# Branch B's gated pair as seven half-size products in front of the heads, its convolution spread over the heads and branch A

## The chip, the core and the metric

The kernel runs on one core of one Trainium2 chip. The metric is the device time of one execution in microseconds (us). The core has a matrix engine (PE, with its own weight loads, PEld), a vector engine (DVE), a scalar engine (ACT) and a general engine (POOL); transfers are issued by SP and POOL through queues. Matrix products here are made of fp32 values split into a high and a low part (`hi`, `lo`, both of type fp32r), and each product is three passes: high by high, high by low, low by high.

## The reference, cut to what matters

512 tokens of 2048 channels go through one layer. Branch B takes two sets of 2048 columns of one large projection, gates one by the sigmoid of the other, and runs a causal convolution of 31 taps over the tokens of each channel:

```python
h = rmsnorm(x, g_pre[i])
proj = h @ w_in[i]
qkv, z_a, b_raw, a_raw, glu_in, z_b, gate_logits = jnp.split(proj, _split_points(), axis=-1)
...
o_a = gated_delta_chunked(q, k, v, g_log, beta)
o_a = rmsnorm(o_a, g_dn_out[i]).reshape(B, S, DN_WIDTH).astype(x.dtype) * jax.nn.silu(z_a)
y_a = o_a @ w_br_a[i]

u = jax.nn.glu(glu_in, axis=-1)
u = causal_depthwise_conv(u, w_dw[i]) + b_dw[i]
u = jax.nn.silu(layernorm(u, ln_g[i], ln_b[i])) * jax.nn.silu(z_b)
y_b = u @ w_br_b[i]

gate_a, gate_b = jnp.split(jax.nn.sigmoid(gate_logits + b_gate[i]), N_BRANCHES, axis=-1)
mixed = (gate_a * y_a + gate_b * y_b) @ w_out[i]
x = x + rmsnorm(mixed, g_post[i])
```

Behind it stands a gated per-layer embedding. `gated_delta_chunked` works on 16 heads of 128 channels in chunks of 64 tokens; each chunk needs the inverse of a 64x64 unit triangular matrix, and a state is carried from chunk to chunk.

## The kernel before

**Two kinds of product.** `gemm_cm` makes one tile of 128 output channels by 512 tokens: 16 pieces of depth 128, three passes each, 48 matmuls. Its weights come as two tiles of 128x1024 (`raw`, loaded by SP), and each half is split by ACT (`nc.scalar.copy`, L127) and DVE (subtraction, L128) into `w`. Seven half-size products in place of eight (Strassen's scheme in Winograd's form) make the projection `w_z` in `z_phase` and, at the end, `w_out`. A round `jp` of `z_phase` makes 512 tokens by 1024 columns: sums of weight blocks come from DVE (`e_a`, `e_b`) and from an accumulating transfer of POOL (`acc`), the sums of the left operand `S1` to `S4` are made once by `form`, and `run` issues the matmuls of two, three and two products, with DVE's additions of the results between them. The result has the tokens on the partitions; `fin` applies SiLU and stores it. There are two rounds. Column block 2jp + 1 of a round is complete after the second `run`, block 2jp after the third.

**The order of the program.** Embedding and transposition of x, five gate tiles, the two rounds of `z_phase`, the tile for beta and decay with its small steps (`beta_decay`), then the heads: eight groups of two heads. A group issues six products (k, q, v of two heads; each followed by a short convolution of four taps, `cv`, three DVE steps, L625) and two products of the queue `rest` (`zb_tile`, `gate_tile`). After the heads come a few more of `rest`, branch A (16 products with `w_br_a`), the layer norm of branch B, branch B's product, `w_out` and the embedding's gate.

**Small work beside the products.** Everything that isn't a product is a generator. `spawn` puts it into a list with a period; `tick` runs once for each matmul of `gemm_cm` and steps a generator whenever its count of matmuls has passed. A generator that yields a number waits for so many matmuls instead. This gives the program order; the build then fixes the order of each engine, with tiles granted from pools, and only instructions that are pinned (`pin`, L811) keep their program order exactly.

**A group of heads**, spawned with period HP = 4, goes through this chain: transposes of k, q, v on PE; `pg` on PE; W on DVE (L780); four copies `Ud` on ACT (L794); `UT` on DVE (L800); 31 pairs `prod` and `VT` on DVE (multiplication L811 and sum L812), which invert the triangular matrices column by column, each pair dependent on the one before; `Vd` (L819); four copies `VP` on ACT and four transposes `Tc` on DVE (L826); then `py` (L832) and `pz` (L835) on PE, which read `Tc`. From these the scan of the two heads follows.

**The gated pair of branch B** is `glu_pair(i)`, two `gemm_cm` products for each of 16 tiles of channels: the gate tile ends in a sigmoid (`evac_glu_b`), the value tile in a multiplication (`evac_glu_a`), and then `dwconv` is spawned with period CP = 6: a first tap on ACT, 30 dependent DVE steps of one tap each (L898, `uc`), the sum over channels `acc` on POOL and a store to `u_dram`. The first pair stands behind the heads, the second in front of branch A, the other 14 between branch A's products, each of which is also followed by one tile of `rest` as long as there are some. `presum`, spawned in branch A with period 10, makes sums of blocks of `w_out` by transfers on POOL's queue. `layer_norm` starts when all 16 channels' `u_dram` are stored.

## Time and profile before

| | us |
|---|---|
| median of 3 runs | 2472.0 (2471.88 to 2473.21) |
| the profiled execution | 2471.8 |
| its span in the trace | 2470.0 |

The span by stage, from the trace's busy times (us):

| stretch of the span | length | PE | DVE | ACT | POOL |
|---|---|---|---|---|---|
| 0 to 94.6: embedding, x, five gate tiles | 94.6 | 87.1 | 72.1 | 53.8 | 2.6 |
| 94.6 to 250.4: two rounds of `z_phase` | 155.8 | 155.6 | 118.9 | 83.0 | 10.2 |
| 250.4 to 1144: decay and the heads' groups up to the last `py` | 893.6 | 893.2 | 633.3 | 491.0 | 66.9 |
| 1144 to 1226: the last scan, tiles of `rest`, the first gated pairs | 82.0 | 82.0 | 57.5 | 42.7 | 12.1 |
| 1226 to 1825: branch A with the other pairs | 599.0 | 599.0 | 485.0 | 162.2 | 119.8 |
| 1825 to 2470: layer norm, branch B, `w_out`, embedding's gate | 645.0 | 633.4 | 378.3 | 275.9 | 7.2 |

In the prediction a row of the page's first part gives, for each engine, busy time, its share of the span and the number of instructions. A row that starts with two times and a colon is a stretch of the span: its length, then busy time and instructions of PE, PEld, DVE, ACT and POOL, the granted clock of PE, the share of time in which the DMA engines were busy, and GB/s. A row that starts with one time is a single instruction, or some alike behind each other: start, duration, engine, line, operation, output and inputs with shape; in brackets the idle time of the engine before it and what ended it. A row of costly groups ends in busy time, mean ns of one, and the idle time before. Rows with a queue name a kind of transfer, its count, size and the median us from issue to landing.

### The profile page before, as it was taken

How to read it: one execution, taken by the hardware profiler on the slowest of the kernel's cores; microseconds unless marked ns; L12 is line 12 of the kernel's file. 1: busy time of each engine (PE TensorE's matmuls, PEld its weight loads, DVE VectorE, ACT ScalarE, POOL GpSimd, SP SyncE). 2: the span in 40 equal slices, each digit the busy share in tenths (PEclk: the TensorE clock that was granted, in tenths of full speed). 3: DMA queues.
4: the chain of work that ended last, by engine and by line, in shares of the span. 5: the costliest groups of instructions: out<-in, count | busy, mean ns of one | idle time of the engine just before them, and what ended most of it. 6: DMA issues, size and time to landing. Idle time of an engine off the chain costs nothing.

```text
span 2470.0 us, 33169 instructions
## 1 busy us (share of the span) xinstructions
PE 2450.4 (99%) x12106; PEld 2019.3 (82%) x12106; DVE 1745.0 (71%) x3276; ACT 1108.5 (45%) x2165; POOL 218.7 (9%) x291
## 2 busy tenths in 40 slices
PE   8999999999999999999999999999999999999998
PEld 7888888888888888888888888888888888788886
DVE  7877767777686776766886877868975755667644
ACT  6555565555645556564422222222224723444532
POOL 0001100100000010000222322310000000000000
PEclk9999999999999999999999999999999999999999
DMA  7576432223232222323676866853353633565552
GB/s 267 171 184 176 126 115 86 98 86 99 73 103 90 86 99 86 99 69 116 180 220 184 234 203 184 237 161 111 104 186 123 209 118 108 213 232 168 197 170 77
DMA packets 131460, 361.31 MB, mean 146 GB/s; under 512 B 14816, under 2 KB 23264, under 8 KB 131296
## 3 DMA queue, kind: packets, MB, share of 16 engines
q1 hardware_dynamic: 112096, 310.94, 37.7%
q0 software_dynamic: 18048, 46.15, 8.1%
q10 hardware_dynamic: 1152, 2.10, 0.3%
q8 instruction: 95, 1.56, 0.3%
q14 instruction: 69, 0.57, 0.1%
HBM read 310.90 MB, written 48.23 MB: 145 GB/s over the span
## 4 chain that ended last, share of the span: by engine, by line
PE 97%; DVE 1%; issue 1%; DMA 1%; ACT 0%; SPq 0%; POOL 0%; DVEq 0%; POOLq 0%; ACTq 0%
PE g L183 24%; PE g L185 24%; PE g L181 23%; PE zp L431 2%; PE zp L429 2%; PE zp L430 2%; PE f L1247 2%; PE f L1248 2%; PE f L1246 2%; PE f L1412 2%; PE f L1411 2%; PE f L1410 2%; PE psB L678 1%; PE psS L684 1%; PE psA L672 1%
## 5 line engine op out<-in xcount | busy, mean ns | idle before, releaser
L183 PE MATMUL g<-hl,w 128*128 128x512 f32 x2064 | 815.6, 395 | 0.0
L185 PE MATMUL g<-hh,w 128*128 128x512 f32 x2064 | 815.3, 395 | 0.0
L181 PE MATMUL g<-hh,w 128*128 128x512 f32 x2064 | 813.6, 394 | 0.0
L127 ACT CAST w<-raw 128x512 fp32r<-128x512 f32 x716 | 438.5, 619 | 732.9 <-PE g L185 626.9
L128 DVE TENSOR_TENSOR w<-raw,w 128x512 fp32r<-128x512 f32 x716 | 503.1, 707 | 281.5 <-ACT w L127 279.3
L185 PEld LDWEIGHTS g<-hh,w 128*128 128x128 f32 x2064 | 388.2, 188 | 77.0 <-DVE w L128 2.7
L183 PEld LDWEIGHTS g<-hl,w 128*128 128x128 f32 x2064 | 388.1, 188 | 76.8 <-issue 1.6
L181 PEld LDWEIGHTS g<-hh,w 128*128 128x128 f32 x2064 | 388.3, 188 | 74.5 <-issue 0.5
L898 DVE SCALAR_TENSOR_TENSOR uc<-sg,vec,uc 128x511 f32<-128x511 f32 (+14 forms) x480 | 351.1, 733 | 14.0 <-ACT uc L895 3.9
L625 DVE SCALAR_TENSOR_TENSOR cv<-g,vec,cv 128x511 f32<-128x511 f32 x144 | 106.1, 737 | 29.0 <-ACT cv L623 28.2
L181 PE MATMUL g<-oh,w 128*128 128x512 f32 x256 | 99.6, 389 | 0.0
L183 PE MATMUL g<-ol,w 128*128 128x512 f32 x256 | 99.6, 389 | 0.0
L185 PE MATMUL g<-oh,w 128*128 128x512 f32 x256 | 99.6, 389 | 0.0
L181 PE MATMUL g<-uh,w 128*128 128x512 f32 x256 | 99.6, 389 | 0.0
L183 PE MATMUL g<-ul,w 128*128 128x512 f32 x256 | 99.6, 389 | 0.0
L185 PE MATMUL g<-uh,w 128*128 128x512 f32 x256 | 99.6, 389 | 0.0
L811 DVE TENSOR_TENSOR prod<-UT,VT 128x2 f32<-128x2 f32 (+30 forms) x248 | 87.2, 352 | 6.6
L966 POOL DMA_DIRECT2D wsum<-in_w_out x96 | 75.4, 850 | 75.0 <-issue 28.5
L1247 PE MATMUL f<-wsp,oph 128*128 128x512 f32 x192 | 75.4, 393 | 0.1
L1246 PE MATMUL f<-wsp,oph 128*128 128x512 f32 x192 | 75.4, 394 | 0.0
L1410 PE MATMUL f<-w,xh 128*128 128x512 f32 x192 | 75.4, 392 | 0.0
L1248 PE MATMUL f<-wsp,opl 128*128 128x512 f32 x192 | 75.2, 392 | 0.0
(363 smaller groups left out, 3386.3 us busy)
## 6 DMA issues: line engine op xcount, KB each, us to landing
raw<-in_w_in SPq DMA_DIRECT2D x258, 512.0 KB, 3.3
wsum<-in_w_out POOLq DMA_DIRECT2D x96, 256.0 KB, 5.7
raw<-in_w_ple_gate SPq DMA_DIRECT2D x40, 512.0 KB, 3.4
raw<-in_w_br_a SPq DMA_DIRECT2D x32, 512.0 KB, 3.8
wo_sums<-wsum POOLq DMA_DIRECT2D x64, 256.0 KB, 4.1
raw<-in_w_br_b SPq DMA_DIRECT2D x32, 512.0 KB, 3.3
raw<-in_w_z SPq DMA_DIRECT2D x22, 512.0 KB, 4.3
rw<-wo_sums SPq DMA_DIRECT2D x20, 512.0 KB, 4.3
```

The source lines that it names most:

```text
L127: nc.scalar.copy(hi, rq)
L128: nc.vector.tensor_tensor(lo, rq, hi.bitcast(F32), ALU.subtract)
L181: mm(ps, wh, rh, start=(k == 0), stop=False)
L183: mm(ps, wh, rl, start=False, stop=False)
L185: mm(ps, wl, rh, start=False, stop=(k == NK - 1))
L625: nc.vector.scalar_tensor_tensor(y[:, s:], ps[:, 0:T - s], vv(w0 + 3 - s), y[:, s:], ALU.mult, ALU.add)
L811: pin(nc.vector.tensor_tensor(pv_, um, vm, ALU.mult))
L898: nc.vector.scalar_tensor_tensor(y[:, s:], u[:, 0:T - s], vv(w0 + TAPS - 1 - s), y[:, s:], ALU.mult, ALU.add)
L1246: mm(ps, lh, wh[:, c], start=kk == 0, stop=False)
L1247: mm(ps, lh, wl[:, c], start=False, stop=False)
L1248: mm(ps, ll, wh[:, c], start=False, stop=kk == 7)
L1410: mm(ps[tt], lh, wh, start=k == 0, stop=False)
```

## The change

The columns of the gated pair get a copy in the layout of `w_z` (`w_glu`): four blocks of 1024 columns, the left half values, the right half their gates. `z_phase` runs four more rounds on them, with the same left operand. In these, the right half of the result goes through the sigmoid on ACT, and the left half is multiplied by it on DVE. The gated value has the tokens on the partitions, and the convolution needs the channels there: `transposed` makes 64 transposes of 128x128 on PE into 16 tiles `ut`, copies them out with ACT (`u0`) and stores them to `u0_dram`, 32 transfers of SP. It runs beside the next round's first products, and for the last round behind the phase.

`glu_pair` and its 32 products are gone. `dwconv` loads its channels from `u0_dram` (SP); its 30 steps (now L909) are the same. Channels 0 to 7 are convolved one after the other as a generator that is spawned behind the tile for beta and decay and ends with the heads, one step each 12 matmuls; channels 8 to 15 as one that is spawned in front of branch A, with a step after 4 and 5 matmuls by turns. `acc` is added on DVE in place of POOL. `rest` is taken in another rhythm: six tiles behind the heads, three in front of branch A, seven after branch A's products and the others later. `presum` goes at period 8 with pauses of 19 in place of 10 and 24.

```diff
-        WZ = A["w_z"]
+        blocks = [(A["w_z"], 0), (A["w_z"], 1)] + [(A["w_glu"], j) for j in range(4)]
...
-            nc.sync.dma_start(raw, WZ[jp, blk, q])
+            nc.sync.dma_start(raw, blocks[jp][0][blocks[jp][1], blk, q])
         def acc(t, jp, blk, q):
-            nc.gpsimd.dma_start(t, WZ[jp, blk, q], accum_op=ALU.add)
+            nc.gpsimd.dma_start(t, blocks[jp][0][blocks[jp][1], blk, q], accum_op=ALU.add)
...
-        for jp in range(2):
+        for jp in range(6):
...
-        for jp in range(2):
+        def transposed(cb, halves_):
+            yield
+            yield
+            for half, two in enumerate(halves_):
+                for c2 in range(2):
+                    ps = gps.tile([P, T], F32, tag="g", name="ut")
+                    for n in range(4):
+                        c = 2 * c2 + n // 2
+                        nc.tensor.transpose(ps[:, n * P:(n + 1) * P], two[n % 2][:, c * P:(c + 1) * P], ident)
+                    yield
+                    o = unit_s("u0")
+                    nc.scalar.copy(o, ps)
+                    for n in range(2):
+                        nc.sync.dma_start(u0_dram[cb + 2 * c2 + n][:, half * 256:half * 256 + 256], o[:, n * 256:n * 256 + 256])
+                    yield
+        for jp in range(6):
+            glu = jp >= 2
             ps = run(("P1", "Q5"), stepper(gen, 2))
+            for _ in gen:
+                pass
...
             for t in range(2):
                 tt_(d[t], ps["P3"][t], d[t], ALU.add)
-                fin(t, 2 * jp + 1, d[t])
                 tt_(s5[t], s5[t], u2[t], ALU.subtract)
-                fin(2 + t, 2 * jp + 1, s5[t])
+                for n, c in ((0, d[t]), (2, s5[t])):
+                    if glu:
+                        nc.scalar.activation(c, c, AF.Sigmoid)
+                    else:
+                        fin(n + t, 2 * jp + 1, c)
             ps = run(("P2", "Q4"))
             for t in range(2):
                 tt_(s1[t], ps["P2"][t], s1[t], ALU.add)
-                fin(t, 2 * jp, s1[t])
                 tt_(u2[t], ps["Q4"][t], u2[t], ALU.add)
-                fin(2 + t, 2 * jp, u2[t])
+                for n, c, g in ((0, s1[t], d[t]), (2, u2[t], s5[t])):
+                    if glu:
+                        tt_(c, c, g, ALU.mult)
+                    else:
+                        fin(n + t, 2 * jp, c)
+            gen = transposed(4 * (jp - 2), (s1, u2)) if glu else iter(())
         finish("form")
         ctx_z.close()
+        spawn(gen, 6)
...
+    cpool = [slots, "s"]
+    def dwconv(i):
+        w0 = V_DW + i * TAPS
+        u = cpool[0].tile([P, T], F32, tag=cpool[1], name="u")
+        nc.sync.dma_start(u, u0_dram[i])
+        yield
+        y = cpool[0].tile([P, T], F32, tag=cpool[1], name="uc")
+        nc.scalar.activation(y, u, AF.Identity, scale=vv(w0 + TAPS - 1), bias=vv(V_BDW + i))
+        yield
+        for s in range(1, TAPS):
+            nc.vector.scalar_tensor_tensor(y[:, s:], u[:, 0:T - s], vv(w0 + TAPS - 1 - s), y[:, s:], ALU.mult, ALU.add)
+            yield
+        if i == 0:
+            acc.append(slots.tile([P, T], F32, tag="s", name="acc"))
+            nc.gpsimd.tensor_copy(acc[0], y)
+        else:
+            nc.vector.tensor_tensor(acc[0], acc[0], y, ALU.add)
+        nc.sync.dma_start(u_dram[i], y)
+        done[0] += 1
+    def convs(channels, waits):
+        n = 0
+        for i in channels:
+            for _ in dwconv(i):
+                yield waits[n % len(waits)]
+                n += 1
+    CONV_H = 8
+    jobs.append(lambda: spawn(convs(range(CONV_H), (12,)), 12, "heads"))
...
-        else:
-            nc.gpsimd.tensor_tensor(acc[0], acc[0], y, ALU.add)
...
-    def evac_glu_a(i):
-        def f(ps):
-            u = sg_t.pop(i)
-            nc.vector.tensor_tensor(u, ps, u, ALU.mult)
-            spawn(dwconv(i, u), CP)
-        return f
-
-    def glu_pair(i):
-        gemm_cm(w_in_tile(GLU_TILE0 + 16 + i), hT, evac_glu_b(i))
-        gemm_cm(w_in_tile(GLU_TILE0 + i), hT, evac_glu_a(i))
-
-    for i in range(4):
+    for i in range(6):
         rest.popleft()()
-    glu_pair(0)
...
-                yield 24
+                yield 19
                 yield from give(a, T2)
                 yield from take(a, B21, True)
-                yield 24
+                yield 19
-    rest.popleft()()
-    glu_pair(1)
+    jobs.append(lambda: spawn(convs(range(CONV_H, NK), (4, 5)), 4, "conv"))
+    for _ in range(3):
-    jobs.append(lambda: spawn(presum(), 10, "presum"))
-    nglu = 2
-        if i + 5 < NK:
+        if i < 7:
             rest.popleft()()
-        if nglu < NK:
-            glu_pair(nglu)
-            nglu += 1
...
-    t = w.reshape(2, 4, 2, P, 2, 2, T).transpose(4, 0, 5, 1, 3, 2, 6)
+    t = w.reshape(2, 4, 2, P, -1, 2, T).transpose(4, 0, 5, 1, 3, 2, 6)
...
+        "w_glu": _sw_tiles(np.concatenate([glu[:, n * D + j * T:n * D + (j + 1) * T] for j in range(4) for n in range(2)], axis=1)),
```

The build's order shows where the convolution now stands. Rows are instructions of one engine in its own order: line, operation, output and inputs by name, shape; line numbers are those of the kernel that is shown. The first place is DVE in the fourth group of heads, in the second half of the inversion. `prod` and `VT` are the inversion's pairs, `w` is the split of a weight half for PE. Before:

```order
L812 TENSOR_REDUCE VT<-prod 128x6
L128 TENSOR_TENSOR w<-raw,w 128x512
L811 TENSOR_TENSOR prod<-UT,VT 128x132
L812 TENSOR_REDUCE VT<-prod 128x6
L811 TENSOR_TENSOR prod<-UT,VT 128x138
L812 TENSOR_REDUCE VT<-prod 128x6
L811 TENSOR_TENSOR prod<-UT,VT 128x144
L812 TENSOR_REDUCE VT<-prod 128x6
L811 TENSOR_TENSOR prod<-UT,VT 128x175
```

And with the change, from the same pair on, `uc` being a step of the convolution:

```order
L840 TENSOR_REDUCE VT<-prod 128x6
L909 SCALAR_TENSOR_TENSOR uc<-u,vec,uc 128x508
L839 TENSOR_TENSOR prod<-UT,VT 128x132
L909 SCALAR_TENSOR_TENSOR uc<-u,vec,uc 128x507
L840 TENSOR_REDUCE VT<-prod 128x6
L128 TENSOR_TENSOR w<-raw,w 128x512
L839 TENSOR_TENSOR prod<-UT,VT 128x138
L909 SCALAR_TENSOR_TENSOR uc<-u,vec,uc 128x506
L840 TENSOR_REDUCE VT<-prod 128x6
L909 SCALAR_TENSOR_TENSOR uc<-u,vec,uc 128x505
L839 TENSOR_TENSOR prod<-UT,VT 128x144
```

Before, `VT` is followed by the next `prod` at once, but for one `w`; with the change a step `uc` stands behind nearly every `prod` and every `VT` of this piece.

The second place is DVE behind the inversion, in the same group: `Vd`, then `Tc`, which PE reads in `py` and `pz`. Before:

```order
L819 STREAM_TRANSPOSE Vd<-VT 128x256
L625 SCALAR_TENSOR_TENSOR cv<-g,vec,cv 128x511
L128 TENSOR_TENSOR w<-raw,w 128x512
L625 SCALAR_TENSOR_TENSOR cv<-g,vec,cv 128x510
L826 STREAM_TRANSPOSE Tc<-VP 32x8x32
L625 SCALAR_TENSOR_TENSOR cv<-g,vec,cv 128x509
L826 STREAM_TRANSPOSE Tc<-VP 32x8x32 x3
```

With the change:

```order
L909 SCALAR_TENSOR_TENSOR uc<-u,vec,uc 128x499
L847 STREAM_TRANSPOSE Vd<-VT 128x256
L128 TENSOR_TENSOR w<-raw,w 128x512
L854 STREAM_TRANSPOSE Tc<-VP 32x8x32 x4
L909 SCALAR_TENSOR_TENSOR uc<-u,vec,uc 128x498
L128 TENSOR_TENSOR w<-raw,w 128x512
```

The three `cv` between `Vd` and `Tc` have moved ahead of `Vd`; the `w` has stayed, and the four `Tc` follow one another. On PE nothing has moved between `pg` and `py` in this group: 190 matmuls `g` and the one `pe` stand there before and with the change.

The third place is DVE in branch A. `gt` is the evacuation of a product of branch A. Before, a product of branch A, a pair of products for the gated pair and the convolution run side by side:

```order
L950 TENSOR_TENSOR gt<-g,gt 128x512
L128 TENSOR_TENSOR w<-raw,w 128x512
L898 SCALAR_TENSOR_TENSOR uc<-sg,vec,uc 128x500
L898 SCALAR_TENSOR_TENSOR uc<-sg,vec,uc 128x499
L898 SCALAR_TENSOR_TENSOR uc<-sg,vec,uc 128x498
L128 TENSOR_TENSOR w<-raw,w 128x512
L898 SCALAR_TENSOR_TENSOR uc<-sg,vec,uc 128x497
L898 SCALAR_TENSOR_TENSOR uc<-sg,vec,uc 128x496
L898 SCALAR_TENSOR_TENSOR uc<-sg,vec,uc 128x495
```

With the change:

```order
L909 SCALAR_TENSOR_TENSOR uc<-u,vec,uc 128x492
L909 SCALAR_TENSOR_TENSOR uc<-u,vec,uc 128x506
L970 TENSOR_TENSOR gt<-g,gt 128x512
L128 TENSOR_TENSOR w<-raw,w 128x512
L909 SCALAR_TENSOR_TENSOR uc<-u,vec,uc 128x491
L909 SCALAR_TENSOR_TENSOR uc<-u,vec,uc 128x505
L909 SCALAR_TENSOR_TENSOR uc<-u,vec,uc 128x490
L128 TENSOR_TENSOR w<-raw,w 128x512
L909 SCALAR_TENSOR_TENSOR uc<-u,vec,uc 128x489
L909 SCALAR_TENSOR_TENSOR uc<-u,vec,uc 128x504
L909 SCALAR_TENSOR_TENSOR uc<-u,vec,uc 128x488
L909 SCALAR_TENSOR_TENSOR uc<-u,vec,uc 128x503
```

Two channels' steps now alternate where one channel's steps followed each other, and three or four stand between two `w` where three stood; the steps of channels 0 to 7 have left this stage, and so have the products of the gated pairs.

More of the change, by code (lines that the diff above doesn't have):

```diff
@@ L267, in _body @@
     zb_dram = dram.tile([NK, P, T], F32, name="zb_dram")
+    u0_dram = dram.tile([NK, P, T], F32, name="u0_dram")
     def gate_tile(i, src=True):
@@ L363, in load @@
                 for n in range(2):
-                    nc.sync.dma_start(two[n], WZ[jp, blk, q][:, n * T:(n + 1) * T])
+                    nc.sync.dma_start(two[n], blocks[jp][0][blocks[jp][1], blk, q][:, n * T:(n + 1) * T])
                 return two
             raw = rawp.tile([P, 1024], F32, tag="raw", name="raw", bufs=3)
-            nc.sync.dma_start(raw, WZ[jp, blk, q])
+            nc.sync.dma_start(raw, blocks[jp][0][blocks[jp][1], blk, q])
             return [raw[:, 0:T], raw[:, T:]]
         def acc(t, jp, blk, q):
-            nc.gpsimd.dma_start(t, WZ[jp, blk, q], accum_op=ALU.add)
+            nc.gpsimd.dma_start(t, blocks[jp][0][blocks[jp][1], blk, q], accum_op=ALU.add)
         def parts(t):
@@ L864, in group @@
             yield wait
+    u_t = [None] * NK
+    done = [0]
+    acc = []
+    cpool = [slots, "s"]
[25 more added lines that the diff above has]
+    jobs.append(lambda: spawn(convs(range(CONV_H), (12,)), 12, "heads"))
     rest = deque([lambda i=i: zb_tile(i) for i in range(NK)] + [lambda i=i: gate_tile(i) for i in range(FILL, NK)]
@@ L989, in load_gate @@
         nc.sync.dma_start(mixed[i], g_dram[i])
-    rest.popleft()()
-    glu_pair(1)
+    jobs.append(lambda: spawn(convs(range(CONV_H, NK), (4, 5)), 4, "conv"))
+    for _ in range(3):
+        rest.popleft()()
     jobs.append(lambda: finish("oa"))
@@ L995, in _body @@
         jobs.append(lambda i=i: load_gate(i))
-    jobs.append(lambda: spawn(presum(), 10, "presum"))
-    nglu = 2
+    jobs.append(lambda: spawn(presum(), 8, "presum"))
     for i in range(NK):
```

27 lines of the change are left out of this document (2 added, 25 removed).

## The prediction

> **What bounds the kernel now.** I read the page's busy times first, then the chain of work that ended last, then the busy times by stage.
>
> ```profile
> PE 2450.4 (99%) x12106; PEld 2019.3 (82%) x12106; DVE 1745.0 (71%) x3276; ACT 1108.5 (45%) x2165; POOL 218.7 (9%) x291
> PE 97%; DVE 1%; issue 1%; DMA 1%; ACT 0%; SPq 0%; POOL 0%; DVEq 0%; POOLq 0%; ACTq 0%
> 94.00:250.00 156.00, 155.76 (x675) 126.32 (x674) 119.08 (x195) 82.58 (x141) 10.15 (x19) 1.00 0.64 178
> 670.00:714.00 44.00, 44.00 (x203) 35.86 (x201) 34.20 (x92) 22.80 (x29) 1.38 (x2) 1.00 0.31 102
> 714.00:778.00 64.00, 64.00 (x443) 53.34 (x442) 42.50 (x103) 36.02 (x112) 5.89 (x7) 1.00 0.26 83
> 1400.00:1600.00 200.00, 200.00 (x884) 165.68 (x883) 158.06 (x228) 54.91 (x88) 56.55 (x78) 1.00 0.75 212
> ```
>
> PE is the bound: 99% busy, 97% of the chain, no stage with idle PE. So work taken off PE is time won, as long as no engine that feeds PE falls behind. The rows by stage (PE, PEld, DVE, ACT, POOL) show who could: DVE. In branch A (1400 to 1600) 884 matmuls start in 200 us, one each 0.226 us; a matmul's own 0.39 us overlaps the next and is not its price.
>
> The average hides one place. A group of two heads holds an inversion, and its run on DVE is this:
>
> ```profile
> 678.97 1.25 DVE L800 STREAM_TRANSPOSE UT<-Ud 128x1024 f32<-128x1024 f32 x1 [6.87 <-ACT Ud L794]
> ...
> 709.06 0.67 DVE L819 STREAM_TRANSPOSE Vd<-VT 128x256 f32<-128x256 f32 x1
> ...
> 712.62 1.38 DVE L826 STREAM_TRANSPOSE Tc<-VP 32x256 f32<-32x256 f32 x3
> ...
> 713.88 0.69 PE L832 MATMUL py<-Tc,W 32*32 32x32 f32 x32
> 714.50 0.68 PE L835 MATMUL pz<-W,Tc 64*64 64x64 f32 x16
> ```
>
> DVE idles 6.87 us for ACT's copies, starts UT at 678.97, works through to Vd at 709.06 (30.1 us) and ends the last Tc at 714.00. PE reads Tc in py and pz, and pz starts at 714.50. PE was not idle, but the spare is 0.50 us. From UT to the last Tc DVE, not PE, has no room.
>
> **The change part by part.** I sum against the profiled execution, 2471.8 us (span 2470.0), 0.2 us under the median of 2472.0.
>
> Removed: 32 products of 48 matmuls, 1536 x 0.2262 = 347.5 us of PE.
>
> Added: four rounds of seven half-size products, 336 matmuls each, of the kind that the z phase has twice.
>
> ```profile
> L429 PE MATMUL zp<-w,hh x66: 389/397/398, 94.6 to 249.6; 128*128 128x512 f32 x66
> L431 PE MATMUL zp<-w,hl x66: 389/393/397, 95.0 to 250.0; 128*128 128x512 f32 x66
> L258 PE MATMUL xp<-cst,x 128*128 128x128 f32 x64 | 8.4, 274 | 0.0
> ```
>
> The z phase's 672 matmuls run from 94.6 to 250.4 with the seams between rounds in it: 155.8 us, 0.232 us each, so 1344 cost 311.7 us. The 64 transposes are as many and as large as those of x: 8.4 us. PE is left 347.5 - 311.7 - 8.4 = **27.4 us** less. In these rounds DVE gets about the z phase's load (119 of 156 us), four multiplications a round more; ACT (83 of 156) and DMA (0.64) have room for the extra copies. If that cover failed I would bound it by what a round lost so far, 77.9 - 336 x 0.2262 = 1.9 us, once more for four rounds: 0 to 8 us; I take 0, because the row's own price holds the seams.
>
> Moved: the convolution, 30 dependent DVE steps a channel. Eight channels go into the heads, eight into branch A, and their order is what matters. In a steady group (third to seventh) the run from UT to Vd has 12 splits w and 3 steps cv before; now 14 w, 6 cv and 13 steps uc stand there (the rows of the change's section are a piece of it). What one costs there, start to start:
>
> ```profile
> 693.42 0.28 DVE L812 TENSOR_REDUCE VT<-prod 128x6 f32<-128x126 f32 x1
> 693.62 0.68 DVE L128 TENSOR_TENSOR w<-raw,w 128x512 fp32r<-128x512 f32 x1
> 694.22 0.40 DVE L811 TENSOR_TENSOR prod<-UT,VT 128x132 f32<-128x132 f32 x1
> 694.66 0.29 DVE L812 TENSOR_REDUCE VT<-prod 128x6 f32<-128x132 f32 x1
> ...
> 697.86 0.74 DVE L625 SCALAR_TENSOR_TENSOR cv<-g,vec,cv 128x511 f32<-128x511 f32 x1
> 698.52 0.68 DVE L128 TENSOR_TENSOR w<-raw,w 128x512 fp32r<-128x512 f32 x1
> 699.12 0.74 DVE L625 SCALAR_TENSOR_TENSOR cv<-g,vec,cv 128x510 f32<-128x510 f32 x1
> ```
>
> A w takes 0.60 us, a cv 0.66; uc is the same instruction on the same width, 0.66. An independent step behind a VT starts 0.08 us before its end, a dependent one 0.04 after (694.22 + 0.40 to 694.66), so each dependent pair that is parted gives 0.12 back; 20 more are parted. Sum: 13 x 0.66 + 3 x 0.66 + 2 x 0.60 - 20 x 0.12 = 9.4 us on a run that had no gap. Behind Vd the three cv are gone, and the four Tc then follow ACT's copies as in the last group, which has no cv either:
>
> ```profile
> 1109.41 1.25 DVE L800 STREAM_TRANSPOSE UT<-Ud 128x1024 f32<-128x1024 f32 x1 [6.86 <-ACT Ud L794]
> ...
> 1137.79 0.67 DVE L819 STREAM_TRANSPOSE Vd<-VT 128x256 f32<-128x256 f32 x1
> ...
> 1141.32 0.44 DVE L826 STREAM_TRANSPOSE Tc<-VP 32x256 f32<-32x256 f32 x1 [0.28 <-ACT VP L825]
> ```
>
> 3.97 us from Vd to the last Tc's end, where a steady group has 4.94: 1.0 us back. PE's side has not moved: 190 matmuls and pe between pg and py, before and after. So pz comes 9.4 - 1.0 - 0.5 = **7.9 us late in a steady group**. Nothing covers it: py heads PE's queue, and every weight product stands behind it. The second group has 14 uc, 15 w and two matmuls more: 8.4. In the first, 26 uc, 19 w and 12 cv add 21.8 us by the same prices, and 53 more matmuls (12.0 us) lie before py: 21.8 - 12.0 - 1.0 - 0.5 = 8.3. The last has no uc. Heads: 5 x 7.9 + 8.4 + 8.3 = **56 us**. The lower bound is half of it, should DVE start its run earlier than in any group seen; the upper adds the rest of each group. There 17 uc and 0.66 us each make 11 us beside 42.5 of 64: 84%, and in the order most stand where DVE waits for PE. I take nothing; at most one step's 0.66 us at a few places, 3 us a group, 20 in all.
>
> Between the z phase and the first group the decay's small steps meet 30 uc (20 us):
>
> ```profile
> 250.00:298.00 48.00, 47.90 (x217) 39.05 (x216) 32.04 (x69) 24.11 (x38) 8.44 (x7) 1.00 0.40 121
> 298.00:347.00 49.00, 48.72 (x244) 39.46 (x244) 34.20 (x59) 32.31 (x71) 7.59 (x8) 1.00 0.39 126
> ```
>
> 66 + 20 of 97 us fits on average, not in every piece; 0 to 8 us, and I take 3.
>
> Branch A: two products (96 matmuls, 21.7 us) now have 25 uc, 8 w and one evacuation or acc: 25 x 0.65 + 8 x 0.60 + 0.68 = 21.7. DVE is exactly full for 20 products. The weights run three pieces ahead (a piece lasts 12 x 0.226 = 2.7 us), so 8 us of lag show nothing: 0 to 10 us, I take 1. The presum is stepped faster, 198 ticks (44.8 us) for a q instead of 248.
>
> ```profile
> wsum<-in_w_out POOLq DMA_DIRECT2D x96, 256.0 KB, 5.7
> wo_sums<-wsum POOLq DMA_DIRECT2D x64, 256.0 KB, 4.1
> ```
>
> Its longest dependent line is four loads and three stores, 4 x 5.7 + 3 x 4.1 = 35 us, which still fits. But it now lasts into the layer norm, and there rst on POOL, gate evacuations on ACT and loads on SP's queue stand behind its landings, with DVE's dg and PE's weights behind them in turn: 0 to 15 us, I take 1, since 35 is well under 44.8.
>
> Sum: 2471.8 - 27.4 + 56.2 + 3 + 1 + 1 = 2505.6, so **2506 us**.
>
> **The rivals.** *The cover holds, faster.* If the 13 steps cost PE nothing, because DVE finishes Tc before py after all, the time is 2471.8 - 27.4 + 5 = 2449. For it speaks that PE never idled in the heads and most uc stand harmlessly; against it the 0.50 us. The point that decides is 9.4 us of added work against 1.5 us of room. Chance 0.16.
>
> *The stall is smaller.* Half of it, 28 us: 2478. It needs room that seven groups lack: 0.09, about half of it within 0.2% of no change.
>
> *The clock drops in the stalls.* Here the two ends of the trace speak:
>
> ```profile
> 7.78 0.63 PE L213 MATMUL e_ps<-w,ph 128*128 128x512 f32 x1
> 8.20 0.63 PE L214 MATMUL e_ps<-w,ph 128*128 128x512 f32 x1
> ...
> 10.68 0.39 PE L214 MATMUL e_ps<-w,ph 128*128 128x512 f32 x1
> 2460.00:2464.00 4.00, 0.71 (x4) 0.23 (x2) 2.10 (x6) 1.57 (x6) 0.55 (x1) 1.00 0.01 2
> 2465.00:2467.00 2.00, 0.00 (x0) 0.00 (x0) 1.31 (x2) 0.00 (x0) 0.00 (x0) 0.50 0.95 327
> ```
>
> The granted clock (the third column from the right) was 1.00 through 2464 and 0.50 from 2465 on, some 4 us after the last two matmuls, and the first matmuls started 0.42 us apart until 10.68. A stall that long would cost ten matmuls 0.2 us each, 2 us; seven of them 14: 2520. A late stall is broken up, since the last splits in the run are late too: by my sums some 1 us, 1.5 us, then 4 us before py and 0.8 before pz, just at the limit. Chance 0.21. [...]
>
> *Branch A or the layer norm stalls.* DVE full or the presum late by the upper bounds above, 10 to 25 us on top: 2523. No wait of that kind is in the trace; chance 0.12.
>
> *The change doesn't do what it says*: the built order shows it does, so nothing is kept for this.
>
> **How the numbers follow.** The forecast keeps 0.42. The range leaves out the faster case (0.16) and a little above its end: 2478 to 2530. A measurement of this kernel can't tell less than about 0.2%, 5 us, from no change. Faster by more than that 0.16, within it 0.05, slower 0.79.
>
> **What would show it.** Right: PE idle in front of py and pz in seven groups, 6 to 9 us each, put down to DVE's Tc, with uc between prod and VT and no idle time on DVE; a group of about 115 us instead of 107.6 (four groups lie between the UT rows at 678.97 and 1109.41); rounds of 78 us in the longer z phase; branch A without idle PE. Wrong: a group that keeps 107.6 us; idle PE mainly in the rounds of seven products or behind the presum's landings; a granted clock under 1.00 inside the heads, which would be the third rival.

## The result, and the profile after

| | before | with the change |
|---|---|---|
| median, us | 2472.07 (2471.88 to 2473.21) | 2538.25 (2537.08 to 2545.23, 4 runs) |
| the profiled execution | 2471.8 | 2545.2, the longest of the four |
| its span | 2470.0 | 2543.4 |

The ratio is 1.0273 (1.0254 to 1.0291): slower by 66 us, 32 us beyond the forecast and 8 beyond the range's upper end.

The page's busy times and its chain of work that ended last, with the change:

```profile
PE 2469.7 (97%) x11978; PEld 2010.4 (79%) x11978; DVE 1861.4 (73%) x3539; ACT 1183.5 (47%) x2299; POOL 222.1 (9%) x292
PE 72%; DVE 19%; issue 4%; DMA 3%; ACT 2%; SPq 0%; POOL 0%; DVEq 0%; POOLq 0%; ACTq 0%
```

PE has 128 instructions fewer and is busy 19 us longer, and a quarter of the chain runs through other engines. What PE waited for, by the view of its waits (total us, times, longest):

```profile
PE py L860 <- DVE Tc L854: 33.9, 12, 5.2
PE g L185 <- DVE w L128: 7.3, 9, 1.2
```

One wait of 5.2 us stands in each steady group. PE's timeline in the fourth group shows it (start, duration, engine, line, operation; in brackets the idle time ahead and who ended it):

```profile
1084.40 0.39 PE L183 MATMUL g<-hl,w 128*128 128x512 f32 x1
1089.95 0.28 PE L860 MATMUL py<-Tc,W 32*32 32x32 f32 x2 [5.16 <-DVE Tc L854]
1090.53 1.06 PE L860 MATMUL py<-Tc,W 32*32 32x32 f32 x30 [0.30 <-DVE Tc L854]
1091.52 2.33 PE L863 MATMUL pz<-W,Tc 64*64 64x64 f32 x32
1093.77 0.79 PE L185 MATMUL g<-hh,w 128*128 128x512 f32 x1
1094.36 0.63 PE L181 MATMUL g<-hh,w 128*128 128x512 f32 x1
...
1097.35 0.55 PE L183 MATMUL g<-hl,w 128*128 128x512 f32 x1
1097.74 0.40 PE L185 MATMUL g<-hh,w 128*128 128x512 f32 x1
```

and DVE's timeline, what PE waited for. DVE has no idle time of 0.1 us or more from UT (1048.68) to Vd, and behind Vd only 0.15 to 0.24 us ahead of each Tc, for ACT's copy:

```profile
1086.41 0.71 DVE L128 TENSOR_TENSOR w<-raw,w 128x512 fp32r<-128x512 f32 x1
1087.02 0.44 DVE L840 TENSOR_REDUCE VT<-prod 128x8 f32<-128x256 f32 x1
1087.35 0.75 DVE L909 SCALAR_TENSOR_TENSOR uc<-u,vec,uc 128x499 f32<-128x499 f32 x1
1087.99 0.65 DVE L847 STREAM_TRANSPOSE Vd<-VT 128x256 f32<-128x256 f32 x1
...
1091.38 0.44 DVE L854 STREAM_TRANSPOSE Tc<-VP 32x256 f32<-32x256 f32 x1 [0.24 <-ACT VP L853]
```

That is the forecast's stall, at its place. But PE's matmuls behind it start 0.43 us apart instead of 0.23 until 1097.4. The busy times by stretch have the granted clock in the third column from the right:

```profile
1086.00:1087.00 1.00, 0.00 (x0) 0.00 (x0) 1.00 (x2) 0.30 (x1) 0.00 (x0) 1.00 0.00 0
1087.00:1088.00 1.00, 0.00 (x0) 0.00 (x0) 1.00 (x4) 0.00 (x0) 0.00 (x0) 0.72 0.85 279
1088.00:1090.00 2.00, 0.05 (x2) 0.08 (x2) 1.65 (x4) 1.30 (x2) 0.70 (x1) 0.50 0.31 123
...
1096.00:1097.00 1.00, 1.00 (x4) 0.73 (x3) 0.88 (x2) 0.00 (x0) 0.00 (x0) 0.50 0.00 0
1097.00:1098.00 1.00, 1.00 (x5) 0.80 (x4) 0.00 (x0) 0.00 (x0) 0.00 (x0) 0.66 0.00 0
1098.00:1099.00 1.00, 1.00 (x7) 0.55 (x5) 0.10 (x1) 0.82 (x2) 0.00 (x0) 1.00 0.00 0
```

The clock fell to half 2.6 us into the wait (1087.44) and stayed there for 10.2 us, far into the work behind it. Added up over the span in stretches of one or two microseconds, PE had 75 us at half clock between the rounds and branch A; before the change, none.

By stage, from matmul starts: the rounds of seven products 476.6 us instead of 155.4; from their end to branch A's first product 1069.0 instead of 976.5; branch A 255.8 instead of 598.2; from its last product to w_out's first 296.8, unchanged.

The following table is worked out from each trace, from the start of pg's last matmul and of py's first; it carries most of the verdicts below. "pg to py" and "py to next pg" are a steady group's (third to seventh) in us, "half" the time at half clock in one such group. The first two groups with the change differ: 13.7 us at half clock in each, and 3.4 more in the first.

| kernel | median, us | pg to py | py to next pg | group | half |
|---|---|---|---|---|---|
| before | 2472 | 44.0 | 63.6 | 107.6 | 0 |
| with the change | 2538 | 50.3 | 67.1 to 68.6 | 117.4 to 118.9 | 6.8 or 10.2 |
| e1, py later | 2545 | 63.2 | 56.3 | 119.5 | 3.4 |
| e2, paused in the inversions | 2485 | 43.9 | 65.7 | 109.7 | 0 |
| e3, wait filled | 2550 | 50.3 | 68.0 | 118.3 | 3.4 or 6.8 |
| e4, before with 13 steps | 2544 | 50.2 | 66.3 to 67.7 | 116.5 to 117.9 | 6.8 |
| e5, before with 5 steps | 2508 | 46.3 | 66.5 | 112.7 | 3.4 |
| e6, before with 9 steps | 2533 | 48.4 | 67.6 | 116.0 | 6.8 or 10.2 |
| e7, no steps | 2455 | 44.0 | 63.6 | 107.6 | 0 |
| e8, moved out | 2486 | 44.0 | 65.5 to 66.3 | 109.5 to 110.3 | 0 |
| e9, 5 steps, wait filled | 2500 | 46.2 | 65.1 | 111.3 | 0 |
| e11, steps ahead of UT | 2494 | 44.7 to 45.0 | 67.1 to 69.3 | 111.8 to 114.0 | 0 or 3.4 |

### The profile page after: what moved, and what is told of

Its sections match the earlier page's. It is cut to its first block, busy times and chain, and to the rows that moved or that the text cites. A ratio compares the mean times of both kernels' runs of the same rounds, so it can differ in the third digit from the quotient of the medians.

```text
span 2543.4 us, 33500 instructions
## 1 busy us (share of the span) xinstructions
PE 2469.7 (97%) x11978; PEld 2010.4 (79%) x11978; DVE 1861.4 (73%) x3539; ACT 1183.5 (47%) x2299; POOL 222.1 (9%) x292
## 4 chain that ended last, share of the span: by engine, by line
PE 72%; DVE 19%; issue 4%; DMA 3%; ACT 2%; SPq 0%; POOL 0%; DVEq 0%; POOLq 0%; ACTq 0%
PE g L185 11%; PE g L183 11%; PE g L181 11%; DVE uc L909 7%; PE zp L430 6%; PE zp L432 6%; PE zp L431 6%; DVE w L128 4%; DVE prod L839 3%; PE f L1264 2%; PE f L1265 2%; DVE VT L840 2%; PE f L1263 2%; PE f L1429 2%; PE f L1428 2%
## 5 line engine op out<-in xcount | busy, mean ns | idle before, releaser
L185 PE MATMUL g<-hh,w 128*128 128x512 f32 x1552 | 624.1, 402 | 6.5 <-DVE w L128 6.5
L181 PE MATMUL g<-hh,w 128*128 128x512 f32 x1552 | 621.6, 401 | 2.9 <-ACT w L127 2.9
L183 PE MATMUL g<-hl,w 128*128 128x512 f32 x1552 | 622.0, 401 | 0.0
L127 ACT CAST w<-raw 128x512 fp32r<-128x512 f32 x588 | 357.1, 618 | 476.8 <-PE g L185 341.0
L128 DVE TENSOR_TENSOR w<-raw,w 128x512 fp32r<-128x512 f32 x588 | 404.1, 691 | 222.7 <-ACT w L127 220.7
L185 PEld LDWEIGHTS g<-hh,w 128*128 128x128 f32 x1552 | 295.9, 191 | 68.9 <-DVE w L128 13.1
L909 DVE SCALAR_TENSOR_TENSOR uc<-u,vec,uc 128x503 f32<-128x503 f32 (+23 forms) x480 | 345.2, 741 | 4.1 <-ACT uc L906 1.6
L181 PEld LDWEIGHTS g<-hh,w 128*128 128x128 f32 x1552 | 296.0, 191 | 59.5 <-ACT w L127 4.2
L183 PEld LDWEIGHTS g<-hl,w 128*128 128x128 f32 x1552 | 295.7, 191 | 57.2 <-issue 1.4
L430 PE MATMUL zp<-w,zoh 128*128 128x512 f32 x256 | 101.7, 397 | 0.0
L432 PE MATMUL zp<-w,zol 128*128 128x512 f32 x256 | 100.7, 393 | 0.0
L431 PE MATMUL zp<-w,zoh 128*128 128x512 f32 x256 | 100.0, 390 | 0.0
L417 ACT CAST w<-zt 128x512 fp32r<-128x512 f32 x96 | 59.3, 621 | 79.9 <-PE zp L432 57.5
```

The source lines that it names most:

```text
L127: nc.scalar.copy(hi, rq)
L128: nc.vector.tensor_tensor(lo, rq, hi.bitcast(F32), ALU.subtract)
L181: mm(ps, wh, rh, start=(k == 0), stop=False)
L183: mm(ps, wh, rl, start=False, stop=False)
L185: mm(ps, wl, rh, start=False, stop=(k == NK - 1))
L430: mm(ps[pr][t], lh, wh, start=q + n == 0, stop=False)
```

## The experiments

**e1: more cover ahead of py.** On the changed kernel, between the last Tc and py:

```diff
-        yield 22
+        yield 82
```

> The changed kernel, but the group's generator waits 82 matmuls instead of 22 between Tc and py and pz; in the built order 250 products g stand between pg and py in groups 2 to 8 instead of 190, with the same 14 w, 6 cv and 13 uc in the inversion's run. Theory A (the lengthened run of DVE makes PE wait at py, and the wait drops the clock): 60 more matmuls are 13.6 us of cover against a wait of 5 us, so groups 2 to 7 lose both the wait and the half clock, some 11 us each: about 2538 - 66 = 2472, down to 2460; only the first group still waits; up to 14 us may come back behind the last group, whose scan ends later. Rival B (the rounds of seven products, the full DVE or the transfers cost the time, the waits at py are only where it shows): PE waits elsewhere instead, over 2520.

Measured: 2545.45 us, ratio to before 1.0300 (1.0285 to 1.0316). The wait at py has gone from all groups but the first, as expected, and the time hasn't. What PE waited for:

```profile
PE psB L706 <- DVE VP L881: 30.7, 6, 5.1
PE g L185 <- DVE w L128: 18.5, 14, 1.7
PE g L181 <- ACT w L127: 8.7, 9, 2.1
```

The wait of 5.1 us has moved to the next instruction that needs DVE in order: VP, the addition behind pd. DVE's timeline from the last Tc to that VP:

```profile
969.64 0.44 DVE L854 STREAM_TRANSPOSE Tc<-VP 32x256 f32<-32x256 f32 x1 [0.26 <-ACT VP L853]
970.11 0.74 DVE L909 SCALAR_TENSOR_TENSOR uc<-u,vec,uc 128x498 f32<-128x498 f32 x1
970.77 0.68 DVE L128 TENSOR_TENSOR w<-raw,w 128x512 fp32r<-128x512 f32 x1
971.37 2.27 DVE L909 SCALAR_TENSOR_TENSOR uc<-u,vec,uc 128x497 f32<-128x497 f32 x3
...
988.76 1.82 DVE L909 SCALAR_TENSOR_TENSOR uc<-u,vec,uc 128x483 f32<-128x483 f32 x2
990.50 0.40 DVE L881 TENSOR_TENSOR VP<-VP,pd 32x256 f32<-32x256 f32 x1
```

From UT (926.03) to this VP DVE has no idle time over 0.3 us: 64 us of work in which steps uc, cv and splits w stand ahead of VP in the queue. Its late w hold PE in the meantime (18.5 us over the run). What stood in DVE's queue made the first thing that PE needed late, 5.1 us at VP, and Theory A's price for this run was wrong: cover at this one reader handed the lateness to the next. The time lies in Rival B's range, and its "full DVE" fits this run; e2 and e4 tell the two apart.

**e2: the steps paused during the inversion.** On the changed kernel; `inv` is set ahead of Ud and cleared behind Tc:

```diff
             for _ in dwconv(i):
                 yield waits[n % len(waits)]
                 n += 1
+                while inv[0]:
+                    yield 2
...
-    jobs.append(lambda: spawn(convs(range(CONV_H), (12,)), 12, "heads"))
+    jobs.append(lambda: spawn(convs(range(CONV_H), (8,)), 8, "heads"))
```

> The changed kernel, but the convolution of channels 0 to 7 pauses from Ud to Tc in each group and is stepped every 8 matmuls otherwise, its steps pinned among the inversion's products; no step uc is left between UT and Vd in groups 2 to 8 (12 w and 3 cv, as before the change), and 26 stand in the rest of each group. Theory A: no wait at py and no drop of the clock in groups 2 to 8; 2538 - 70 to 85, so 2453 to 2470, if DVE has room for 26 steps (17 us) in the rest of a group, where it is busy 42.5 of 64 us. Rival B (the full DVE in the whole of the heads): the same work only moves, the waits come back at the weights; over 2510.

Measured: 2485.24 us, ratio 1.0055 (1.0040 to 1.0070), 53 us of the 66 back with the same 480 steps, though 15 us above Theory A's range. The steady groups have neither wait nor half clock; but a group keeps 2.1 us above 107.6, with no single wait over 0.3 us: 26 steps outside the inversions cost 0.08 us each on average. The rest is in the first group (a wait of 4.1 and one of 3.05 us) and in branch A (260.0 us).

**e3: the wait filled with matmuls.** On the changed kernel, ahead of py:

```diff
+        for n in range(12):
+            mm(pz.rearrange("p x i -> p (x i)"), hT[n][0][:, 0:P], hT[0][0], start=True, stop=True)
```

> The changed kernel with 12 more matmuls of 128x512 (2.7 us) on PE right ahead of py in each group, their result overwritten; nothing is taken away. Theory C (the idle time itself costs 53 us and the clock that falls to half in it another 40): the idle time shrinks from 5.2 to 2.5 us, the granted clock stays 1.00 and py starts when it did: about 3.7 us less in groups 2 to 7, some 20 to 35 us less in all, 2503 to 2518, although 96 matmuls were added. Rival D (the clock in the record costs nothing): py starts when it did or later, 2538 to 2560.

Measured: 2550.06 us, ratio 1.0317 (1.0301 to 1.0332). py starts when it did and the time at half clock is down to 3.4 or 6.8 us a group, but not to none, and a group is no shorter: in the two groups with 3.4 us psB waits 0.9 us for DVE's VP. There PE at full clock waited for DVE's next result. The time lies in Rival D's range, so in the changed kernel this run doesn't show that the clock costs anything; its price comes from e9. Between the two profiled spans (2549.2 and 2543.4 us) nearly all of the difference lies in branch A, 261.4 against 255.8 us, with one wait of 4.1 us for weights; what made that wait is left open. The medians lie 12 us apart, since the profiled execution of the changed kernel was its longest.

**e4, e5, e6: the suspected cost alone.** On the kernel before the change, steps of the convolution's kind in the last pairs of each inversion, 13 here (`j < 10` for 5 steps, `j < 18` for 9):

```diff
+        jt = slots.tile([P, T], F32, tag="s", name="jt")
+        nc.gpsimd.memset(jt, 0.0)
...
             nc.vector.tensor_reduce(VT[:, j, i0:8], pv_, AX, ALU.add)
+            if j % 2 == 0 and j < 26:
+                pin(nc.vector.scalar_tensor_tensor(jt[:, 1:], cst[:, 0:T - 1], vv(V_DW), jt[:, 1:], ALU.mult, ALU.add))
```

> The kernel before the change, with nothing but 13 steps of the convolution's kind (on a tile that nobody reads) among the last pairs of each group's inversion; 3 cv and a w move into the run with them. Theory A: each group waits at py as in the changed kernel, 7 to 8 us of lateness and 3.5 of half clock: 8 x 11 = 88 us, a little less in the last group, which has 2.5 us of room: 2545 to 2562. Rival B: the run has hidden room or the waits come from the rest of the change; 2472 to 2500.

> As the run with 13 added steps on the kernel before the change, with 5 instead. Theory A: by the same prices 5 x 0.66, 3 cv and a w more, less the parted pairs, the 1.0 us behind Vd and the room of 0.5 us: 3.3 us late in each group, idle time too short for the clock to fall: 8 x 3.3 = 26 us less the last group's room, 2493 to 2498, and no time at half clock. Theory C' (any wait at py drops the clock): as above and 3 us a group, 2515 to 2522. Rival B: 2472 to 2476.

> As before with 9 steps: 5.6 us late in each group, 43 us in all, 2515 without a drop of the clock. With the drop in every group 2530 to 2540; a time between says that it falls in some groups only. With the runs of 5 and 13 steps the time per step says whether the price is straight or has a step in it.

Measured: 2544.17 us with 13 steps, ratio 1.0295 (1.0278 to 1.0312); 2508.03 with 5, 1.0146 (1.0130 to 1.0161); 2532.79 with 9, 1.0245 (1.0229 to 1.0260). Theory A holds and Rival B falls: 13 steps at this place, with nothing else of the change, cost 72 us. By the starts of pz, PE came 2.9, 5.1 to 5.4 and 6.8 to 7.2 us late, near the prices from single rows (3.3, 5.6, and 7 to 8 us). But the time per step isn't straight: 36 us for 5, 25 more for the next 4, 11 more for the last 4. The clock differs with it: added up, 24, 58 and 55 us at half rate. In three groups of the run with 13 steps 2.0 us of the wait already fall on a late w, ahead of py, and the clock falls 0.2 to 0.8 us behind that short wait:

```profile
499.52 0.62 PE L185 MATMUL g<-hh,w 128*128 128x512 f32 x1 [2.01 <-DVE w L128]
```

In the run with 5 steps the idle time ahead of py is only 2.26 us, and the clock falls all the same, which Theory A had ruled out; 2508 us lies between its 2493 to 2498 and the 2515 to 2522 of Theory C'. PE's timeline of that run, and its busy times by stretch:

```profile
618.47 0.22 PE L836 MATMUL py<-Tc,W 32*32 32x32 f32 x2 [2.26 <-DVE Tc L830]
619.05 0.69 PE L836 MATMUL py<-Tc,W 32*32 32x32 f32 x30 [0.36 <-DVE Tc L830]
619.72 0.33 PE L839 MATMUL pz<-W,Tc 64*64 64x64 f32 x2
620.39 1.48 PE L839 MATMUL pz<-W,Tc 64*64 64x64 f32 x30 [0.35 <-DVE Tc L830]
621.81 0.79 PE L185 MATMUL g<-hh,w 128*128 128x512 f32 x1
```

```profile
619.00:620.00 1.00, 0.95 (x32) 0.76 (x32) 0.54 (x2) 0.95 (x3) 0.00 (x0) 1.00 0.00 0
620.00:621.00 1.00, 0.65 (x21) 0.61 (x22) 0.80 (x2) 1.00 (x2) 0.00 (x0) 1.00 0.06 16
621.00:622.00 1.00, 1.00 (x19) 0.88 (x14) 0.83 (x2) 0.84 (x4) 0.00 (x0) 0.51 0.00 0
622.00:624.00 2.00, 2.00 (x5) 1.61 (x6) 0.00 (x0) 1.07 (x2) 0.00 (x0) 0.50 0.85 248
624.00:625.00 1.00, 1.00 (x5) 0.77 (x5) 0.00 (x0) 0.00 (x0) 0.00 (x0) 0.79 0.08 29
```

From 619 to 620 PE is 95% busy with matmuls of 32x32, and at 621 the clock falls, 4.8 us after the last full matmul's end. The small py and pz did not hold the clock up here.

The run with 9 steps shows when the clock fell. Its seven groups with a drop have the same wait, 4.2 to 4.3 us ahead of py, and the same 8.1 us without a full matmul. Yet the fall comes 4.7 to 5.3 us after the last full matmul in the first four (6.8 us at half rate) and 2.0 us after it in the other three (10.2 us). What fits is a grid: in each of the 14 traces all falls and rises of the clock lie whole multiples of 3.4133 us apart, to 0.002 us. I counted the matmuls of 128x512 that start in each piece of that grid, up to 2440 us of each trace; a busy piece has 15. All 79 falls stand at the end of a piece with at most 6; of the pieces with at most 2, 57 of 71 were followed by a fall; of the 9560 with 7 or more, none. So in these traces the fall came by the place of a wait on the grid, 2.0 to 5.3 us after the last full matmul in this run, and not at a fixed time after it. A group of the run with 5 steps is 33 pieces long (112.7 us), so its seven drops are one place on the grid met seven times.

**e7: the change without the convolution's steps.**

```diff
-        for s in range(1, TAPS):
+        for s in range(1, 1):
```

> The changed kernel without the 480 DVE steps of the convolution (only its first tap on ACT, the sums and the stores stay): the output isn't the layer's. Theory A: all that the change lost is tied to the place of these steps: the saving of 27 us on PE stands bare, 2443 to 2450. Rival E (the rounds of seven products and the transfers cost time of their own, so branch A keeps its late weights at a DMA share of 0.87): 2452 to 2465, with branch A at 255 to 260 us instead of 251.

Measured: 2454.51 us, ratio 0.9930 (0.9916 to 0.9945). The groups are back at 107.6 us. By stage (length, then busy PE, PEld, DVE, ACT, POOL): rounds, rounds to branch A, branch A:

```profile
94.70:571.70 477.00, 472.40 (x2065) 382.27 (x2064) 362.43 (x585) 238.00 (x413) 24.10 (x35) 1.00 0.61 173
571.70:1556.10 984.40, 980.34 (x5601) 808.28 (x5600) 684.01 (x1669) 541.20 (x1224) 79.83 (x96) 1.00 0.33 106
1556.10:1807.20 251.10, 250.85 (x1105) 206.78 (x1104) 77.58 (x115) 64.97 (x107) 76.78 (x111) 1.00 0.87 253
```

Branch A takes 251.1 us at the same DMA share, 0.87, so its late weights come from the steps and not from the transfers: Rival E falls there. But the time lies in Rival E's range, and its other half holds: the bare change gains 17.5 us, not 27. The rounds take 3.6 us more than their price and the stretch behind them 5.8 more than its matmuls: 1.7 us ahead of the first pg, and 4.3 from the last pg to branch A, with a wait of 2.0 us and a drop of the clock.

**e8: no steps up to the first Tc, more of them behind the heads.** e2 with `inv = [True]` at the start, `CONV_H = 6`, and channels 6 to 15 spawned behind two tiles of `rest` after the last group, every 5 matmuls.

> The paused form once more, with the pause also in force from the start to the first group's Tc (no step in the decay's stretch nor in the first inversion), channels 0 to 5 in the heads every 8 matmuls, and channels 6 to 15 from behind the last group on, every 5 matmuls. Theory A: the stretch of the decay and the first group give back some 10 us each, so about 2465 (2460 to 2472), faster than the kernel before the change. Rival F (DVE is full between the inversions, so that a group of 26 steps keeps its 109.7 us, and branch A its late weights): 2473 to 2482.

Measured: 2486.00 us, ratio 1.0053 (1.0036 to 1.0070). Rival F holds, 4 us beyond its range: a group keeps its 2 us, branch A takes 256.8 us, the convolution ends two products later, the layer norm starts 49 us behind branch A's last product instead of 13, and branch B's first product waits 5.8 us for weights, at half clock behind it. What the first stretch gave back was spent there.

**e9: e5 with its wait filled**, 10 matmuls ahead of py as in e3.

> The run with 5 added steps, and 10 matmuls of 128x512 (2.3 us, their result overwritten) on PE right ahead of py, where PE waits 2.26 us in each group. Theory C (the wait together with the small py and pz leaves PE without full matmuls for over 5 us, and only that drops the clock, 3.4 us at half rate in each group): py starts when it did, the clock stays 1.00, a group takes 111.0 instead of 112.7 us: 2494 to 2499 against 2508, although 80 matmuls were added; in the last group, which has no wait, they cost 2 us. Rival D (the clock isn't to blame for any time): 2508 to 2526.

Measured: 2499.57 us, ratio 1.0113 (1.0096 to 1.0129): 8.5 us faster than e5 with 80 matmuls more. py starts when it did (46.2 us after pg in both), and PE's busy times by stretch show the clock at 1.00 through py and pz:

```profile
616.00:618.00 2.00, 1.28 (x41) 1.05 (x42) 1.33 (x4) 1.95 (x4) 0.00 (x0) 1.00 0.00 0
618.00:620.00 2.00, 2.00 (x33) 1.75 (x30) 1.15 (x2) 1.91 (x5) 0.00 (x0) 1.00 0.31 49
620.00:622.00 2.00, 2.00 (x10) 1.52 (x9) 0.00 (x0) 0.92 (x3) 0.00 (x0) 1.00 0.54 213
```

Theory C holds here: these groups, 111.3 us long, meet the grid at different places, and none has a drop. The price of one drop here is 112.7 - 111.3 = 1.4 us for 3.4 us at half rate. How much the small matmuls count stays open: the clock held over a piece with one full matmul and 64 small ones (726.7 to 730.1), and fell in the run with 5 steps behind pieces with none and 45 to 60.

**e10: part of the convolution on POOL.** e8 with channels 0 to 3 on POOL in the heads, and 4 to 7 on DVE:

```diff
+            if i < POOL_C:
+                nc.gpsimd.tensor_scalar(tp[:, s:], u[:, 0:T - s], vv(w0 + TAPS - 1 - s), None, ALU.mult)
+                nc.gpsimd.tensor_tensor(y[:, s:], y[:, s:], tp[:, s:], ALU.add)
```

> The form moved out of the inversions, with channels 0 to 3 on POOL in the heads (a multiplication and an addition for each tap, one tap each 28 matmuls), channels 4 to 7 on DVE between the inversions every 12 matmuls, and channels 8 to 15 behind the heads as before. Theory A: 18 DVE steps in a group instead of 26 and a shorter stage behind: a group of 108 to 109 us, and the late end of the convolution in front of the layer norm is gone: 2462 to 2472, at or under the kernel before. Rival G (POOL's steps, 1.3 us each, delay its small work for the heads, or hold up DVE at a shared resource): 2480 to 2520, with PE waiting for POOL or DVE in the scans.

Measured: 2689.93 us, ratio 1.0883 (1.0866 to 1.0899). Rival G holds, beyond its range. One tap takes POOL 1.71 + 1.30 us; the decay's tiles `tg`, which POOL makes, come up to 12 us late; and three groups take 156 to 163 us. SP's queue is one place where that is made, by the view of its waits:

```profile
SPq L925 <- POOL uc L914: 209.8, 4, 61.2
```

SP waits up to 61 us to store a channel that POOL hasn't finished, and the loads of the weights stand behind that store; in one of the long groups ACT waits 44.7 us for them. DVE's `prod` also took 0.434 us on average instead of 0.352 in e8.

**e11, e12: steps in DVE's own idle time.** e8 with each u loaded a channel ahead, and 8 steps of each group in the program between Ud and UT, where DVE waited 6.87 us; UT pinned behind them:

```diff
+        in_gap(8)
         yield
         VT = hd.tile([P, 32, 8], F32, tag="VT", name="VT", bufs=1)
...
-        nc.vector.transpose(UTf, Ud.rearrange("p s r x -> p (s r x)"))
+        pin(nc.vector.transpose(UTf, Ud.rearrange("p s r x -> p (s r x)")))
```

> The form moved out of the inversions (no step in the decay's stretch nor in an inversion), with 7 channels in the heads: 7 to 8 steps of each group stand ahead of UT, where DVE waited 6.87 us for ACT's copies before the change, the others are made every 11 matmuls outside; 9 channels behind the heads; and each channel's u is loaded one channel ahead, so that ACT's first tap needn't wait for it. Theory A (a step costs only where PE soon reads what stands behind it): the steps ahead of UT are free, 20 steps in the scans cost what 26 cost by the piece, 1.6 us a group; branch A at 251 to 255 us as the loads no longer hold ACT: 2464 to 2474. Rival F (DVE's load itself): a group stays at 109.7 us, branch A at 256 to 260: 2478 to 2488.

> The same with 6 channels in the heads (every 13 matmuls beside those ahead of UT) and 10 behind. Theory A: a group 0.4 us shorter than with 7 channels, branch A and the layer norm later by up to 9 us, since the convolution ends two products later: 2465 to 2480. Rival F: 2475 to 2486.

Measured: 2494.33 us (1.0091, 1.0073 to 1.0109) and 2494.30 us (1.0091, 1.0075 to 1.0107). Both lie above the ranges of Theory A and Rival F. In groups 2 to 7 of e11 UT came 2.6 us later and py 0.7 to 1.0 us later than before the change, and a group takes 112 to 114 us, more than in e8. The steps didn't overrun the idle time; DVE's timeline in the fourth group of e11 shows what did:

```profile
1006.86 4.55 DVE L917 SCALAR_TENSOR_TENSOR uc<-u,vec,uc 128x494 f32<-128x494 f32 x6
1015.20 0.69 DVE L128 TENSOR_TENSOR w<-raw,w 128x512 fp32r<-128x512 f32 x1 [3.78 <-ACT w L127]
1015.81 0.72 DVE L917 SCALAR_TENSOR_TENSOR uc<-u,vec,uc 128x488 f32<-128x488 f32 x1
1016.44 1.24 DVE L830 STREAM_TRANSPOSE UT<-Ud 128x1024 f32<-128x1024 f32 x1
```

A split w now stands ahead of the pinned UT. It needs ACT's cast, which ACT makes behind the four copies Ud and one other, so that DVE idles 3.78 us with steps and UT behind it. Steps in truly idle time, with no w between them and UT, weren't tried. ACT no longer waits for a load of u (54 us of its waits in e8), and branch A takes 255.9 us as before; so the loads weren't its cost either; the steps themselves are what is left, by exclusion.

No placing that was tried brings the 480 steps in for less than the 31 us between e7 and e2, and the bare change gains 17.5. None beats the kernel before.

## Why the prediction was right in direction and 32 us short

**PE's saving.** Forecast 27.4 us. The rounds cost 3.2 us more than 311.7 + 6.3 us (48 of the 64 transposes fall among them), within the bound of 0 to 8 for the seams; I had taken 0. The 5.8 us that e7 loses behind the rounds, which no term held, are met only in part in the changed kernel: the stretch from the last pg to branch A takes 126.1 us before and after, where e7 takes 130.4.

**The stall in the heads.** The mechanism was right, with its place, and the size nearly: pz comes 50.3 - 44.0 later by py, and 1.57 - 0.62 = 0.95 more behind py, 7.3 us in a steady group where 7.9 was forecast; by the same count 8.7 in the second (8.4) and 8.0 in the first (8.3). Together 53 instead of 56 us. e2 and e4 confirm it from both sides: the steps taken out of the run, the stall is gone; put into the kernel before, it is there.

**The clock: the step that failed.** The sum had no term for it. It was a rival, at 2 us in each of seven groups and a chance of 0.21, by the argument that "a late stall is broken up" into pieces of 1, 1.5 and 4 us before py. The trace shows 0.86 us for a late w, 16 us earlier, and then one piece of 5.2 us: DVE's late work stands in a row ahead of Tc. And "the limit", some 4 us after the last matmul, was one fall at the end of one trace. The fall didn't come at a fixed time: in e6 it came 2.0 to 5.3 us after the last full matmul, by the grid, and in e4 a wait of 2.0 us was enough. Nor did the half rate end when work was back: it lasted for whole pieces of 3.4 us, up to four (13.7 us) in a group of the changed kernel. The 75 us at half clock are 22 such pieces; at e9's 1.4 us each that is 31 us, where the rival had 14 and the forecast 0.

These 31 us are an upper value. With the matmuls taken out that moved between its stretches, the heads of the changed kernel lost 86.5 us from the first pg to the last, 33 us beyond the stall, and these 33 hold the clock and the other steps together; by e2's price these steps would be some 10 us. In its own trace the steady groups with three pieces take 118.3 to 118.9 us and those with two 117.4 and 118.0: about 1 us for the third piece. The clock's share is thus 22 to 31 us by these estimates, and e3 shows why no run splits it off cleanly: some of DVE's own lateness lies under it.

**Behind the stall nothing was added: within its bound.** 17 more steps in the rest of a group had 0, and 3 us as the bound. e2's 2.1 us for 26 steps make it 1.4 us a group for 17, if they cost alike; in the changed kernel it can't be told from the clock.

**The decay's stretch** had 3 us: beyond its matmuls it lost 3.9, of which PE waits for DVE 2.8 us (r_ps and gc_ps); 1.7 us are lost in e7 too. **Branch A** had 1 us with a bound of 10: 255.8 instead of 250.7 (598.2 less the 347.5 us of removed products), of which e7 leaves 0.4. **The presum and the layer norm** had 1: from branch A's last product to branch B's first it is 122.7 us before and after.

The sum, with what was measured in place of what was taken, by stretch: -27.4 + 3.2 (rounds) + 3.9 (decay) + 53.2 (stall) + 33.3 (clock and other steps) + 5.1 (branch A) = 71.3, against 73.4 between the two profiled spans. The 2.1 us that are left lie ahead of the rounds (1.1 us less) and behind w_out's first product (3.2 more, with one drop of the clock), where no term stood. The profiled execution is the longest of the four; the others are 6 to 8 us shorter at a mean granted clock of 0.985 to 0.987 instead of 0.984, and what differs in them no trace shows.

The rival "the cover holds" (2449) wasn't near either, even with the inversions freed: e2 came to 2485, since the steps cost 31 us even there (e2 less e7).

## What to carry to other kernels

Work for an engine with idle time wasn't free where it stood in one queue with a chain that the bound engine waited for: DVE was 71% busy, and 13 steps in each inversion cost 72 us (e4). Price such work at its place, by what stands ahead of the next thing that is read. More cover for that reader moved the wait to the next one (from 5.2 us at py to 5.1 at psB, e1); moving the work out of the chain took the wait away (e2). And a wait of PE had a second price here, the half clock. The clock fell behind waits of 2.0 us (e4) and behind each 9.0 us without a full matmul in the changed kernel's steady groups; it stayed at 1.00 over 4.4 us that 38 transposes of 128x128 filled near the changed kernel's start (31.8 to 36.2). The same wait cost 6.8 or 10.2 us at half clock by its place on a grid of 3.4 us (e6), which the forecast couldn't know. In a steady group one to three such pieces followed a wait of 2 to 5 us, at 1.0 to 1.4 us each; the first groups had up to five.

## What the hardware showed that wasn't expected

- The granted clock fell after 2.26 us of idle time followed by 3.3 us that were mostly matmuls of 32x32 and 64x64 (e5), and 10 full matmuls in that idle time kept it at 1.00 and made the kernel 8.5 us faster (e9).
- In each trace the clock changed on a grid of 3.413 us; all 79 falls ended a piece of it with at most 6 starts of 128x512 matmuls, where a busy piece has 15. The same wait of 4.2 us cost 6.8 or 10.2 us at half clock by its place on the grid (e6).
- One split w that needs ACT, ahead of a pinned instruction in DVE's queue, held it for 3.78 us in the middle of "idle" time (e11).
- A multiplication by a column on POOL took 1.71 us on average on 128x511 and a little less, and an addition 1.30 (e10), where one DVE step of both took 0.74 (e2); with these steps on POOL, the mean of DVE's `prod` was 0.434 us (e10) instead of 0.352 (e8).
